# A first phase in fixed order on three engines, and a denser schedule of the late modulation chunks

## The chip, the cores and the metric

The kernel runs on one core of one Trainium2 chip. The metric is the device time of the whole program in microseconds: each run gives one time, and the median over the runs is quoted. Profiled executions give, beside their time, a trace of all engines.

The engines are TensorE (PE in the profile, with its weight loads as PEld), VectorE (DVE), ScalarE (ACT), GpSimd (POOL) and SyncE (SP), which only issues DMAs here.

## The reference

One layer of a diffusion backbone, on 256 latent tokens `x` and 256 context tokens `ctx`, model width 2048, float32 throughout. Cut to what matters:

```python
mod = (silu(c) @ w_mod + b_mod)                    # 6 x 2048: sa, ca, ga, sm, cm, gm
mod_c = (silu(c_ctx) @ w_mod + b_mod)              # only sa_c, ca_c are used
h_c = rmsnorm(ctx, norm_attn_w) * (1 + ca_c) + sa_c
h   = rmsnorm(x,   norm_attn_w) * (1 + ca)   + sa
k_c, v_c = h_c @ w_in[K, V]                        # keys normalized per head
q, k, v, pool_in, gates = h @ w_in                 # q, k normalized, then axial rope
a = softmax(q k^T / 8)[even] - lam * softmax(...)[odd]     # 8 heads, keys of latent and context
y_a = rmsnorm(a @ v) * (1 - lam_init) @ w_a_up
y_b = multiscale_pool(pool_in) @ w_b_up
x = x + ga * ((sigmoid(g_a) * y_a + sigmoid(g_b) * y_b) @ w_o)
x = x + gm * (relu((rmsnorm(x) * (1 + cm) + sm) @ w_ff1) ** 2 @ w_ff2)
```

## The kernel before, in words

**Precision.** Every float32 product with a large weight is made of three matmuls in a reduced format: weight and activation are each split into a high part (a cast on ScalarE) and a low part (a subtraction on VectorE), and high x high, high x low and low x high are summed. A 512 KB weight chunk therefore costs one cast and one subtraction of 128 x 1024 before TensorE uses it.

**Loading.** `stream` is the list of all weight chunks in the order of use, filled by `plan` at the head of the program. `wchunk` gives out the next chunk, and first issues loads on SP's queue until a few chunks lie ahead (`AHEAD` 2, in the first phase `FIRST_AHEAD` 6). Raw chunks go to a few rotating buffers, so SP's queue stops where a buffer is still in use.

**Order.** The program is written as one stream of operations; a planner with its own cost model and priorities puts them into an order for each engine. Operations that go through `pin` keep their written order among themselves. The wrappers `act` and `vec` pin everything while `ordered[0]` is true, and `pe` while `ordered_pe[0]` is true. In the first phase only `ordered_pe` is set before the change.

**First phase.** It computes sa and ca for latent and context, the modulated activations of both, and for the first four heads the keys of latent (`kx`) and context (`kc`) and the queries of latent (`q`), for one 128-row feature tile f of 16 after the other. For each f: `mod_tile(f)` multiplies four raw chunks of w_mod by the two conditioning vectors (32 matmuls) and transposes the result in blocks on VectorE (`blocks`); `features(f)` turns it upright on TensorE (`modT`, L67) through `mod_columns`, scales the activations on VectorE (`hw`), adds the shift on ScalarE for the high part (`hL`, `hC`) and on VectorE for the low part (`hidden`); `product(n, f)` is six matmuls for each of kx, kc, q. `keep` splits a chunk of w_k and w_q at every even f. The norm of the latent tokens is taken at the start; that of the context (`context_squares`, `context_norm`, with one matmul into `ssq`) behind `mod_tile(2)`. Features lag one tile behind mod tiles, context products two. `tables()` makes the rope tables and lambda, behind f = 10. Six PSUM banks accumulate through all of the phase.

**Later phases.** Behind it come values (`v_group(0)`), the other half of queries, keys and values, pooling, and then `gates()`, beside attention as a side generator; then w_o in four column groups of eight chunks; then the MLP. On the way from w_o to the MLP stands a chain: `projected` (xtmp, x, x1sq), `norm2`, `shifted`, transposes `hidden2` (h2T), and the first products in `ff1_first`, written for the first half of the tokens ahead of the second.

**Late modulation.** ga, cm, sm and gm (latent only) are computed on VectorE in the shadow of the later phases: `late_gen` is a generator that at each call loads one 512 KB chunk and orders a multiply-add into `macc` (L624); behind the 16 chunks of each of eight halves comes a sum over partitions on TensorE (`late`, L643). Calls are handed out by credit: each weight chunk in `stream` carries a `rate`, `load_next` adds it to `credit`, and each whole credit is one call. Behind w_o, `while "gm" not in mods: next(late[0])` makes all calls that are still missing for ga, cm and sm.

Of the kernel before, what the change touches and what calls it, by code (L numbers as in the profile page):

```python
# [14 lines left out]
ALU = mybir.AluOpType  # L15
AX = mybir.AxisListType

P = 128
D = 2048
KT = D // P  # L20
T = 256
# [27 lines left out]
def layer(ctx: ExitStack, tc, a, out):  # L49
# [5 lines left out]
    ordered = [False]  # L55
    ordered_pe = [False]
# [12 lines left out]
    act, vec, pe, sp = Engine(nc.scalar, ordered), Engine(nc.vector, ordered), Engine(nc.tensor, ordered_pe), nc.sync  # L69
# [4 lines left out]
    def work(name, shape=None, dt=F32):  # L74
        return pool.tile(shape or [P, 512], dt, tag="w2", name=name, bufs=9)
# [13 lines left out]
    late = [None]  # L89
    credit = [0.0]  # L90
# [33 lines left out]
    stream = []  # L124

    def plan(name, *idx, rate=0.0):
        stream.append(((name,) + idx, rate))
# [3 lines left out]
    for f in range(KT):  # L131
        for i in range(4):
            plan("w_m", f, i)
            if (f, i) == (9, 0):
                plan("prq")
        if f == 1:
            for i in range(4):
                plan("cT", i)
        if f % 2 == 0:
            plan("w_k", 0, f // 2)  # L140
            plan("w_q", 0, f // 2)
    for n, g, rate in (("w_v", 0, 1.5), ("w_q", 1, 1.0), ("w_k", 1, 1.5), ("w_v", 1, 1.5)):
        for ch in range(8):
            plan(n, g, ch, rate=0.0 if (n, g) == ("w_v", 1) and ch < 3 else rate)
    for g in range(4):
# [4 lines left out]
    for g in range(4):  # L150
        for n, nk in (("w_gb_in", 8), ("w_b", 4), ("w_ga_in", 8), ("w_a", 4)):
            for ch in range(nk):
                plan(n, g, ch, rate=0.55)
                if g == 0 and n == "w_gb_in" and ch in (1, 7):
                    plan("pool_w", 2 if ch == 1 else 3)
    for g in range(4):
        for ch in range(8):
            plan("w_o", g, ch, rate=0.25 if g < 3 else 0.0)
            if g == 0:
                plan("x", ch // 4, ch % 4)  # L160
    for b in range(9):
        if b == 0:
            for k in range(KT):
# [8 lines left out]
    FIRST_AHEAD = 6  # L172
# [9 lines left out]
    done = [0]  # L182
# [12 lines left out]
    def load_next():  # L195
        key, rate = stream[len(loaded)]
        src = a[key[0]]
        for i in key[1:]:
            src = src[i]
        if key[0] == "prq":  # L200
            nc.sync.dma_start(prq, src)
            loaded.append((key, None, None))
            return
        if key[0] in ("cT", "x"):
            dst = cT[:, 4 * key[1]:4 * key[1] + 4, :] if key[0] == "cT" else x1_tile()[:, key[1], key[2] * 512:key[2] * 512 + 512]
            nc.sync.dma_start(dst, src)
            loaded.append((key, None, None))
            return
        n = src.shape[-1]
        if key[0] == "w_m":  # L210
            raw = mod_raw(*key[1:])
            sp.dma_start(raw, src)
            loaded.append((key, raw, raw))
            return
        if key[0] in ("w_k", "w_q") and key[1] == 0:
            raw = pool.tile([P, n], F32, tag="aT", name="raw", bufs=2)
            sp.dma_start(raw, src)
            loaded.append((key, raw, raw))
            return
        raw = raw_chunk(src, n)  # L220
        if key == ("w_ff1a", 0):
            hi, lo = (pool.tile([P, n], F32R, tag="aT", name=nm, bufs=2) for nm in ("hi0", "lo0"))
        elif key == ("w_ff1a", 1):
            halves = [[work(nm, dt=F32R) for nm in ("hi1", "lo1")] for _ in range(2)]
            for h in range(2):
                split(*halves[h], raw[:, h * 512:h * 512 + 512])
            loaded.append((key, *zip(*halves)))
            return
        else:
            hi = pool.tile([P, n], F32R, tag="whi", name="whi", bufs=3)  # L230
            lo = pool.tile([P, n], F32R, tag="wlo", name="wlo", bufs=3)
        act.copy(hi, raw)  # L232
        vec.tensor_sub(lo, raw, hi.bitcast(F32))  # L233
        loaded.append((key, hi, lo))
        credit[0] += rate
        credit_rate[0] = rate
        while credit[0] >= 1.0:
            credit[0] -= 1.0
            if late[0] is not None:
                next(late[0], None)  # L240

    def wchunk(*key, ahead=AHEAD):
        while len(loaded) < min(done[0] + 1 + ahead, len(stream)) or loaded[done[0]][1] is None:
            if loaded and done[0] < len(loaded) and loaded[done[0]][1] is None:
                done[0] += 1
                continue
            load_next()
        got, hi, lo = loaded[done[0]]
        assert got == key, (got, key)
        loaded[done[0]] = None  # L250
        done[0] += 1
        tick()
        return hi, lo

    def split(hi, lo, src):
        act.copy(hi, src)
# [23 lines left out]
    xT = s16("xT", [P, KT, T])  # L280
    cT = s16("cT", [P, KT, T])
# [67 lines left out]
    hL = [pairtile("hL0")]  # L349
    hC = [pairtile("hC0")]  # L350
# [10 lines left out]
    def mod_tile(f, ps):  # L361

        raws = [wchunk("w_m", f, i, ahead=FIRST_AHEAD)[0] for i in range(4)]
        c = (f % 2) * T
        for i in range(4):
            for j in range(4):
                k = 4 * i + j  # L370
                pe.matmul(ps[32 * j:32 * j + 32, c:c + T], cv[:, k, :], raws[i][:, j * T:j * T + T],
                          start=k < 4, stop=k >= 12)
        blocks = work("blocks", [P, T])
        vec.transpose(blocks, ps[:, c:c + T])
        return blocks.rearrange("p (a g r) -> p a g r", a=2, g=4)
# [11 lines left out]
        vec.tensor_scalar(c3[:, 0, :], c3[:, 0, :], pr("nw")[:, f:f + 1], None, ALU.mult)  # L387
        return c3

    def hidden(f, t, c3):  # L390

        src, h = ((xT, hL), (cT, hC))[t]
        u = work("hw", [P, T])
        ht, k8 = h[f // 8], f % 8
        bias = c3[:, 1, t:t + 1]
        vec.scalar_tensor_tensor(u, src[:, f, :], c3[:, 0, t:t + 1], rms[t], ALU.mult, ALU.mult)
        act.activation(ht[:, 0, k8, :], u, AF.Identity, bias=bias)
        vec.scalar_tensor_tensor(ht[:, 1, k8, :], u, bias, ht[:, 0, k8, :].bitcast(F32), ALU.add, ALU.subtract)

# [81 lines left out]
    def product(n, k):  # L481

        w = "w_q" if n == "q" else "w_k"
        if w not in fb:
            fb[w] = [bank(f"{w}_{t}") for t in range(4 if n != "q" else 2)]
        hi, lo = held[w, k // 2]
        kk = k % 2
        for t in range(2):
            t4 = t + (2 if n == "kc" else 0)
            xmm([fb[w][t4]], [tokens(4)[t4]], k, hi, lo, slice(kk * 512, kk * 512 + 512), k == 0, k == KT - 1)  # L490
# [13 lines left out]
            total.append(sq[0])  # L504


    ordered_pe[0] = True
    sb = bank("ssq")
    for i in range(4):
        square_sums(xT, vec, sb, i)()  # L510
# [3 lines left out]
    def features(f):  # L514

        if f == 8:
            hL.append(pairtile("hL1"))
            hC.append(pairtile("hC1"))
        cols[f] = mod_columns(f, blocks[f])
        hidden(f, 0, cols[f])  # L520
        for k in (0, 1, 2) if f == 2 else (f,) if f > 2 else ():
            hidden(k, 1, cols[k])

    def context_norm():

# [6 lines left out]
    def keep(w, j, raw):  # L532

        if w == "w_k":
            if not first:
                first.append(s16("first", [P, 4, 1024], F32R))
            i = 2 * (j % 2)
            held[w, j] = first[0][:, i, :], first[0][:, i + 1, :]
        else:
            held[w, j] = [pool.tile([P, 1024], F32R, tag=tag, name=tag, bufs=3) for tag in ("whi", "wlo")]  # L540
        split(*held[w, j], raw)

    for f in range(KT):
        if f % 2 == 0:
            ps = bank("mod")
        if f > 0:
            features(f - 1)
        blocks[f] = mod_tile(f, ps)
        if f == 2:
            for i in range(4):  # L550
                context_squares(i)
            context_norm()
        if f > 0:
            product("kx", f - 1)
        if f == 4:
            for k in range(2):
                product("kc", k)
        if 3 < f < KT - 1:
            product("kc", f - 2)
        if 0 < f < KT - 1:  # L560
            product("q", f - 1)
        if f % 2 == 0:
            for w in ("w_k", "w_q"):
                keep(w, f // 2, wchunk(w, 0, f // 2, ahead=FIRST_AHEAD if f < 14 else 1)[0])
        if f == 10:
            tables()
    features(KT - 1)
    product("kc", KT - 3)
    product("q", KT - 2)
    product("kc", KT - 2)  # L570
    for n in ("kx", "q", "kc"):
        product(n, KT - 1)
    ordered_pe[0] = False
    kb, qb = fb["w_k"], fb["w_q"]
    qT = s8("qT", [P, NH, T])
    kT = s16("kT", [P, NH, 2 * T])
# [591 lines left out]
```

## Time and profile before

| | |
|---|---|
| runs | 1484.52, 1485.43, 1487.09 us, median 1485.43 |
| profiled execution | 1486.54 us, its span 1484.7 us |
| busy in the span | PE 1444.8, PEld 1186.5, DVE 998.6, ACT 686.1, POOL 120.3 us |
| loaded from HBM | 344.45 MB |
| mean granted TensorE clock | 0.989 |

The span runs from the first to the last instruction of the trace; the execution's own time lies 1.8 us above it. Busy times of different engines overlap. In the lines below, a row of waits reads "engine line waited for: us in total, times, longest us"; a row of the chain "start, us, what"; a row of the timeline "start, us, engine line op out<-in xcount [idle before <-what ended it]". All are microseconds from the start of the span. A helper's line (L67, L256, L257) stands for many callers, so tiles are named as well.

### The profile page before, as it was taken

The numbers are of one execution on the slowest core, as the hardware profiler recorded it, in microseconds if no ns is written. First come the engines' busy times: TensorE is split into PE (matmuls) and PEld (weight loads), VectorE is DVE, ScalarE is ACT, GpSimd is POOL, SyncE is SP. The second block draws the span as 40 slices with busy tenths as digits, with TensorE's granted clock in tenths as the row PEclk, the third lists the DMA queues.
The fourth block names the chain that finished last, engine by engine and source line by source line (L and its number), as shares of the span: only waits on it lengthen the run. The fifth ranks groups of instructions, "written<-read, shape, count | busy, mean of one in ns | idle before, by whom it ended". The sixth has DMA issues, their size and how long they took to land.

```text
span 1484.7 us, 19763 instructions
## 1 busy us (share of the span) xinstructions
PE 1444.8 (97%) x7466; PEld 1186.5 (80%) x7466; DVE 998.6 (67%) x1243; ACT 686.1 (46%) x929; POOL 120.3 (8%) x120
## 2 busy tenths in 40 slices
PE   5899999999999999999989999999999999999998
PEld 2567887778888888888858888888888888888887
DVE  3557686858888677777786765666666555555675
ACT  4224345456654444444434545535445453544432
POOL 0000101002400000000000100100000000000260
PEclk8899999999999999999999999999999999999999
DMA  9896494334688888897756677767777565565564
GB/s 378 349 390 257 148 321 156 128 118 159 198 305 300 301 285 286 294 322 249 236 194 215 227 238 239 236 221 236 243 233 247 188 187 196 185 196 188 186 198 141
DMA packets 97439, 347.85 MB, mean 234 GB/s; under 512 B 11072, under 2 KB 11712, under 8 KB 97344
## 3 DMA queue, kind: packets, MB, share of 16 engines
q1 hardware_dynamic: 96768, 345.51, 68.7%
q8 instruction: 58, 0.95, 0.3%
q0 software_dynamic: 576, 1.08, 0.2%
q14 instruction: 37, 0.30, 0.1%
HBM read 344.45 MB, written 2.10 MB: 233 GB/s over the span
## 4 chain that ended last, share of the span: by engine, by line
PE 91%; DVE 4%; DMA 3%; ACT 1%; issue 1%; POOL 0%; SPq 0%; DVEq 0%; ACTq 0%; POOLq 0%
PE f L1017 14%; PE f L427 8%; PE f L426 8%; PE f L429 8%; PE f L1020 7%; PE pg L426 4%; PE pg L427 4%; PE pg L429 4%; PE w_k L67 3%; DMA raw<-in_w_m_dram 2%; PE pyy L426 2%; PE pyy L427 2%; PE pyy L429 2%; PE wo L426 2%; PE wo L427 2%; PE wo L429 2%
## 5 line engine op out<-in xcount | busy, mean ns | idle before, releaser
L233 DVE TENSOR_TENSOR wlo<-raw,whi 128x1024 fp32r<-128x1024 f32 (+1 forms) x433 | 540.0, 1248 | 355.7 <-ACT whi L232 330.7
L232 ACT CAST whi<-raw 128x1024 fp32r<-128x1024 f32 (+1 forms) x433 | 453.3, 1047 | 558.8 <-PE f L427 178.5
L1017 PE MATMUL f<-h,whi 128*128 128x512 f32 x896 | 224.3, 392 | 0.0
L427 PE MATMUL f<-whi,act 128*128 128x512 f32 x512 | 199.3, 389 | 0.0
L426 PE MATMUL f<-whi,act 128*128 128x512 f32 x512 | 199.3, 389 | 0.0
L1017 PEld LDWEIGHTS f<-h,whi 128*128 128x128 f32 x896 | 161.6, 189 | 29.2
L624 DVE SCALAR_TENSOR_TENSOR macc<-raw,sil,macc 128x1024 f32<-128x1024 f32 x128 | 163.9, 1280 | 1.1 <-DMA raw<-in_w_sm_dram 0.7
L429 PE MATMUL f<-wlo,act 128*128 128x512 f32 x512 | 136.8, 389 | 0.0
L1020 PEld LDWEIGHTS f<-h,wlo 128*128 128x128 f32 x896 | 122.2, 190 | 8.7
L1020 PE MATMUL f<-h,wlo 128*128 128x256 f32 x896 | 124.9, 282 | 0.0
L429 PEld LDWEIGHTS f<-wlo,act 128*128 128x128 f32 x512 | 96.1, 188 | 19.9
L427 PEld LDWEIGHTS f<-whi,act 128*128 128x128 f32 x512 | 96.1, 188 | 19.9
L426 PEld LDWEIGHTS f<-whi,act 128*128 128x128 f32 x512 | 96.1, 188 | 19.8
L426 PE MATMUL pg<-whi,hL 128*128 128x512 f32 x256 | 100.7, 393 | 0.0
L427 PE MATMUL pg<-whi,hL 128*128 128x512 f32 x256 | 99.7, 389 | 0.0
L1028 POOL TENSOR_TENSOR rsq<-relu 128x512 f32<-128x512 f32 x28 | 29.1, 1040 | 538.7 <-ACT relu L1027 518.4
L429 PE MATMUL pg<-wlo,hL 128*128 128x512 f32 x256 | 68.4, 389 | 0.0
L427 PEld LDWEIGHTS pg<-whi,hL 128*128 128x128 f32 x256 | 48.1, 188 | 10.2 <-issue 0.2
L426 PEld LDWEIGHTS pg<-whi,hL 128*128 128x128 f32 x256 | 48.1, 188 | 10.2 <-ACT whi L232 0.2
L429 PEld LDWEIGHTS pg<-wlo,hL 128*128 128x128 f32 x256 | 48.0, 188 | 10.0
L426 PE MATMUL wo<-whi,mix 128*128 128x512 f32 x116 | 45.2, 390 | 0.0
L427 PE MATMUL wo<-whi,mix 128*128 128x512 f32 x116 | 45.1, 389 | 0.0
(269 smaller groups left out, 2050.2 us busy)
## 6 DMA issues: line engine op xcount, KB each, us to landing
raw<-in_w_ff_dram SPq DMA_DIRECT2D x240, 512.0 KB, 4.2
raw<-in_w_m_dram SPq DMA_DIRECT2D x64, 512.0 KB, 8.9
raw<-in_w_ga_dram SPq DMA_DIRECT2D x32, 512.0 KB, 4.5
raw<-in_w_cm_dram SPq DMA_DIRECT2D x32, 512.0 KB, 4.7
raw<-in_w_gb_in_dram SPq DMA_DIRECT2D x32, 512.0 KB, 4.7
raw<-in_w_ga_in_dram SPq DMA_DIRECT2D x32, 512.0 KB, 4.8
raw<-in_w_sm_dram SPq DMA_DIRECT2D x32, 512.0 KB, 4.6
raw<-in_w_o_dram SPq DMA_DIRECT2D x32, 512.0 KB, 4.5
```

The source lines that it names most:

```text
L67: return (lambda *a, **k: pin(emit(*a, **k))) if self.flag[0] else emit
L232: act.copy(hi, raw)
L233: vec.tensor_sub(lo, raw, hi.bitcast(F32))
L426: pe.matmul(banks[t], tok(h, k, 0, tt), wt, start=k == 0, stop=False)
L427: pe.matmul(banks[t], tok(h, k, 1, tt), wt, start=False, stop=False)
L429: pe.matmul(banks[t], tok(h, k, 0, tt), wt, start=False, stop=k == 2 * nk - 1)
L624: pin(vec.scalar_tensor_tensor(acc, raw, sil[:, 0, k:k + 1], acc, ALU.mult, ALU.add))
L1017: pe.matmul(ps, hi[:, kk * P:kk * P + P], both(h2, k), start=k == 0, stop=False)
L1020: pe.matmul(ps[:, T:2 * T], lo[:, kk * P:kk * P + P], act_slice(h2, k, 0), start=False, stop=k == KT - 1)
L1028: gp.tensor_mul(sq, r, r)
```

## The change

It touches the first phase and the rates.

- In the first phase ScalarE and VectorE keep the written order too, not TensorE alone.
- The context tokens cT are loaded behind the first modulation tile instead of the second, and their squares and norm stand behind `mod_tile(0)` instead of `mod_tile(2)`.
- Features of tile f stand behind the products of tile f - 1 at the end of a step, for latent and context together; the context product lags one tile, as the others do. Tile 0 has its latent features first and its context features (`hidden_context`) behind the split of the first w_k and w_q chunks; kx and q of tile 0 stand in step 0, kc of tile 0 in step 1.
- `tables()` stands behind f = 11 instead of 10.
- `first_chunk` loads no chunk of the next phase ahead.
- Credit is collected only once the generator exists. The rate of the first w_v group is 0.75 instead of 1.5, that of gates 0.6 instead of 0.55, that of w_o 0.5 in two column groups instead of 0.25 in three. x is loaded two pieces per column group of w_o instead of all eight in the first.

```diff
-        if f == 1:
+        if f == 0:
             for i in range(4):
                 plan("cT", i)
...
-    for n, g, rate in (("w_v", 0, 1.5), ("w_q", 1, 1.0), ("w_k", 1, 1.5), ("w_v", 1, 1.5)):
+    FIRST_LOADS = len(stream)
+    for n, g, rate in (("w_v", 0, 0.75), ("w_q", 1, 1.0), ("w_k", 1, 1.5), ("w_v", 1, 1.5)):
...
-                plan(n, g, ch, rate=0.55)
+                plan(n, g, ch, rate=0.6)
...
-            plan("w_o", g, ch, rate=0.25 if g < 3 else 0.0)
-            if g == 0:
-                plan("x", ch // 4, ch % 4)
+            plan("w_o", g, ch, rate=0.5 if g < 2 else 0.0)
+            if ch % 4 == 0:
+                plan("x", ch // 4, g)
...
-        credit[0] += rate
+        credit[0] += rate if late[0] is not None else 0.0
...
+    def first_chunk(*key):
+        return wchunk(*key, ahead=min(FIRST_AHEAD, FIRST_LOADS - done[0] - 1))[0]
...
-    def hidden(f, t, c3):
-
-        src, h = ((xT, hL), (cT, hC))[t]
+    def hidden(f, c3):
+
+        us = []
+        for t, src in enumerate((xT, cT)[:len(rms)]):
+            u = work("hw", [P, T])
+            vec.scalar_tensor_tensor(u, src[:, f, :], c3[:, 0, t:t + 1], rms[t], ALU.mult, ALU.mult)
+            us.append(u)
+        for t, u in enumerate(us):
+            add_shift(f, t, u, c3)
+
+    def hidden_context(f, c3):
+
         u = work("hw", [P, T])
-        ht, k8 = h[f // 8], f % 8
+        vec.scalar_tensor_tensor(u, cT[:, f, :], c3[:, 0, 1:2], rms[1], ALU.mult, ALU.mult)
+        add_shift(f, 1, u, c3)
+
+    def add_shift(f, t, u, c3):
+
+        ht, k8 = (hL, hC)[t][f // 8], f % 8
         bias = c3[:, 1, t:t + 1]
-        vec.scalar_tensor_tensor(u, src[:, f, :], c3[:, 0, t:t + 1], rms[t], ALU.mult, ALU.mult)
         act.activation(ht[:, 0, k8, :], u, AF.Identity, bias=bias)
         vec.scalar_tensor_tensor(ht[:, 1, k8, :], u, bias, ht[:, 0, k8, :].bitcast(F32), ALU.add, ALU.subtract)
...
-    ordered_pe[0] = True
+    ordered_pe[0] = ordered[0] = True
...
-        hidden(f, 0, cols[f])
-        for k in (0, 1, 2) if f == 2 else (f,) if f > 2 else ():
-            hidden(k, 1, cols[k])
+        hidden(f, cols[f])
...
-        if f > 0:
-            features(f - 1)
         blocks[f] = mod_tile(f, ps)
-        if f == 2:
+        if f == 0:
+            features(0)
             for i in range(4):
                 context_squares(i)
             context_norm()
-        if f > 0:
-            product("kx", f - 1)
-        if f == 4:
-            for k in range(2):
-                product("kc", k)
-        if 3 < f < KT - 1:
-            product("kc", f - 2)
-        if 0 < f < KT - 1:
-            product("q", f - 1)
+        elif f == 1:
+            product("kc", 0)
+            features(1)
+        else:
+            for n in ("kx", "q", "kc") if f < KT - 1 else ("kx", "q"):
+                product(n, f - 1)
         if f % 2 == 0:
             for w in ("w_k", "w_q"):
-                keep(w, f // 2, wchunk(w, 0, f // 2, ahead=FIRST_AHEAD if f < 14 else 1)[0])
-        if f == 10:
+                keep(w, f // 2, first_chunk(w, 0, f // 2))
+        if f == 0:
+            hidden_context(0, cols[0])
+            product("kx", 0)
+            product("q", 0)
+        if f > 1:
+            features(f)
+        if f == 11:
             tables()
-    features(KT - 1)
-    product("kc", KT - 3)
-    product("q", KT - 2)
-    product("kc", KT - 2)
-    for n in ("kx", "q", "kc"):
-        product(n, KT - 1)
-    ordered_pe[0] = False
+    for n, k in (("kc", KT - 2), ("kx", KT - 1), ("q", KT - 1), ("kc", KT - 1)):
+        product(n, k)
+    ordered_pe[0] = ordered[0] = False
```

More of the change, by code (lines that the diff above doesn't have):

```diff
@@ L238, in load_next @@
             credit[0] -= 1.0
-            if late[0] is not None:
-                next(late[0], None)
+            next(late[0], None)
     def wchunk(*key, ahead=AHEAD):
@@ L361, in mod_tile @@
     def mod_tile(f, ps):
-        raws = [wchunk("w_m", f, i, ahead=FIRST_AHEAD)[0] for i in range(4)]
+        raws = [first_chunk("w_m", f, i) for i in range(4)]
         c = (f % 2) * T
```

## The prediction

> **What bounds the kernel now.** I read the busy line of the page first, then TensorE's waits over the whole span, then busy time by stretches around those waits, then the chain of work and the timeline there.
>
> ```profile
> PE 1444.8 (97%) x7466; PEld 1186.5 (80%) x7466; DVE 998.6 (67%) x1243; ACT 686.1 (46%) x929; POOL 120.3 (8%) x120
> ...
> PE ssq L67 <- DVE sq L527: 7.7, 1, 7.7
> PE ssq L67 <- DVE sq L474: 6.9, 1, 6.9
> PE mod L67 <- DMA raw<-in_w_m_dram: 6.3, 8, 2.2
> PE h2T L932 <- DVE yt L67: 4.3, 2, 3.6
> PE qkT L461 <- ACT e L697: 2.5, 1, 2.5
> ```
>
> TensorE bounds the kernel: 1444.8 of 1484.7 us, so all idle time is 39.9 us. An edit that removes no matmul can win only that, and the time matmuls run at half clock behind an idle stretch. Two places hold most of it: the first phase (the ssq and mod waits) and the passage from w_o to the MLP (h2T). The qkT wait lies in attention, which the change leaves alone.
>
> ```profile
> 34.00:42.00 8.00, 0.32 (x5) 0.16 (x1) 7.42 (x11) 3.11 (x4) 0.00 (x0) 0.50 1.03 410
> 42.00:47.00 5.00, 5.00 (x12) 3.94 (x13) 1.27 (x3) 0.98 (x2) 0.00 (x0) 0.51 1.03 409
> ...
> 750.00:760.00 10.00, 6.87 (x28) 4.69 (x26) 7.89 (x10) 3.38 (x8) 1.44 (x2) 1.00 0.91 344
> 760.00:770.00 10.00, 6.93 (x19) 4.56 (x20) 7.73 (x19) 4.12 (x8) 0.00 (x0) 0.66 0.00 1
> ...
> GB/s 150 344 415 418 412 407 411 403 411 411 410 407 407 412 405 241 28 368 403 417 412 404 393 389 316 395 401 375 398 414 404 407 412 411 346 57 224 68 90 98
> ...
> 33.14 1.05 PE L67 MATMUL mod<-raw,cv 128*32 128x256 f32 x8 [0.64 <-DMA raw<-in_w_m_dram]
> ```
>
> Columns of the windows: length, busy time of PE, PEld, DVE, ACT, POOL, granted clock, DMA share, GB/s. From 34 to 42 us TensorE stands still while VectorE squares the context (sq L527 ends the wait), and the five us behind it run 12 matmuls at clock 0.51, 0.42 us each. The GB/s row covers 0 to 150 us in 40 slices of 3.75 us: about 410 GB/s, with one hole near 60 us (28), where buffers still held by late products blocked the loads. At 410 GB/s a 512 KB chunk takes 1.28 us. The mod row says that chunk 22.3 in queue order (prm counted 0.3) has landed by 33.1 us: the stream starts at about 4.6.
>
> ```profile
> 108.75 0.18 PE modT L67 x8
> ...
> 119.90 1.36 PE w_q L67 x6
> 121.26 0.17 PE modT L67 x8
> ...
> 127.65 1.75 PE mod L67 x32
> ...
> 138.19 1.36 PE w_k L67 x6
> 139.55 0.23 PE v L426
> ```
>
> These are pieces of the chain. Two steps of f take 121.26 - 108.75 = 12.51 us: 6.255 each, all TensorE's (a mod tile 1.75, three products of 1.36, modT 0.18, remainder between them). The last mod tile starts at 127.65 and the value projection at 139.55: I measure the first phase by that start.
>
> **The change, first phase.** cT's four chunks move on SP's queue ahead of w_k, w_q and the second modulation tile, which land 4 x 1.28 = 5.1 us later. The whole phase loads 88.9 chunks: 4.6 + 88.9 x 1.28 = 118.4 us for the last one if the queue never stalls, against a mod tile that now starts at 127.65. So loads leave room, and the question is when TensorE gets into its 6.255 us steps.
>
> ```profile
> 17.25 0.48 DVE L396 SCALAR_TENSOR_TENSOR hw<-xT,col,rms 128x256 f32<-128x256 f32 x1
> 17.57 1.04 ACT L256 CAST whi<-raw 128x1024 fp32r<-128x1024 f32 x1 [2.89 <-DMA raw<-in_w_q_dram]
> 18.65 1.22 DVE L257 TENSOR_TENSOR wlo<-raw,whi 128x1024 fp32r<-128x1024 f32 x1 [0.92 <-ACT whi L256]
> 29.63 3.21 ACT L499 ACTIVATE sq<-cT 128x512 f32<-128x512 f32 x6
> 39.57 0.68 DVE L502 TENSOR_TENSOR sq<-sq 128x512 f32<-128x512 f32 x1
> 41.87 1.19 PE L67 MATMUL ssq<-sq,mean 128*128 128x256 f32 x2 [7.68 <-DVE sq L527]
> 45.07 0.42 DVE L273 SCALAR_TENSOR_TENSOR rms<-rq_t,rms 128x256 f32<-128x256 f32 x1
> 121.50 0.16 DVE L386 TENSOR_TENSOR col<-modT,prm 128x4 f32<-128x4 f32 x1 [3.48 <-PE modT L67]
> 123.42 0.48 DVE L398 SCALAR_TENSOR_TENSOR hC<-hw,col,hC 128x256 fp32r<-128x256 f32 x1
> ```
>
> *Start.* Latent features of tile 0 stay where they are: hw at 17.25, hL on ScalarE until 18.3. In fixed order the eight squares of cT follow: 8 x 0.535 (3.21 / 6) ends at 22.6, behind the last cT chunk (4.6 + 12.3 x 1.28 = 20.3). The last adds take about 2.2 behind it: 24.8. From ssq's start to rms ready the rows give 45.49 - 41.87 = 3.6: 28.5. The two casts of w_k and w_q queue behind that on ScalarE, the two subtractions on VectorE end at 28.5 + 2 x 1.22 = 30.9, and hC of tile 0 at 32.4. TensorE, idle until w_k's split, takes kx and q of tile 0 at half clock: five matmuls of 0.42 from 29.7 (31.8), six more, 34.3. Then mod(1). The row of 42 to 47 shows about 5 us of half clock behind an idle stretch; here, with waits in the window, I take it to last until 38: mod(1) at 2 x 1.75 = 3.5 ends at 37.8. At full clock follow kc(0) 1.36, modT 0.18, mod(2) 1.75, three products 4.08, modT 0.18: mod(3) starts at 45.4. It has landed by 4.6 + 28.3 x 1.28 = 40.8.
>
> *The clock.* The Trainium skill, page "TensorE: Matmul & The Clock Gate", section "What's actually happening", gives full speed after one busy window of about 3.4 us. The 42 to 47 row disagrees with it by some 1.6 us; by the rule full clock would come at 29.7 + 3.4 = 33.1, mod(1) would end at 35.5, and the total be some 2.3 us lower than my sum.
>
> *Steps.* mod(15) would start at 45.4 + 12 x 6.255 = 120.5. In a step VectorE's features last from 121.50 to 123.90, 2.4 us, then come the transpose (0.44), and in even steps two subtractions (2.44): all within 6.255, so fixed order costs nothing there; if w_q came over about 1 us late behind its modulation tile, the features behind it would be late by the rest. One step does not fit:
>
> ```profile
> 87.81 0.18 DVE L328 COPY wkt<-prq 128x64 f32<-128x64 f32 x1
> ...
> 89.17 0.28 DVE L339 TENSOR_TENSOR tabs<-prq 128x32 f32<-128x32 f32 x2
> ...
> 99.18 0.32 DVE L343 TENSOR_TENSOR lm<-prq 128x64 f32<-128x64 f32 x2
> ...
> 101.05 0.15 DVE L347 TENSOR_SCALAR nlam<-nlam 128x1 f32<-128x1 f32 x1
> ```
>
> tables() is 1.64 us (87.81 to 89.45), plus 0.65 for lm and its sum, 0.35 for nlam and a round trip to ScalarE's Exp, say 0.7: 3.3. Now it was put into gaps in two places; in fixed order it stands behind features(11), with transpose(12), two subtractions and features(12) queued behind it. Features 2.7 after modT, tables 6.0, transpose 6.4, casts (behind Exp on ScalarE) and subtractions 9.0, hL(12) 10.3, where kx(12) is due at 6.255 + 1.9 = 8.2: TensorE waits 2.1. Bounds: 0 if that tile has slack, 3.3 if all of it shows. So mod(15) starts at 122.6.
>
> *Tail.* Behind mod(15): 1.75, kx and q of 14 (2.72), modT 0.18, kc(14) in the shadow of the features (1.9), three last products 4.08: 10.6 us, value projection at 133.2. Gain 139.55 - 133.2 = 6.3; bounds 0, if the steps lose it, and 11.3, if clock and tables cost nothing (rivals). The w_v loads, no longer issued from within the phase, stand behind the last w_m and land from 118.4 on, 15 us before use; their casts queue behind hC(15) on ScalarE, with 4 us in hand. I take 0, at most 1 of loss.
>
> **The change, late modulation.** Counting credit: before, six w_v chunks are loaded while there is no generator, so calls by the end of w_o are 3 + 8 + 12 + 7.5 + 8 + 96 x 0.55 + 24 x 0.25 = 97.3. gm exists at call 103, so six are forced behind w_o, five of them with a load and a multiply-add. After: 6 + 8 + 12 + 7.5 + 8 + 96 x 0.6 + 8 x 0.5 = 103.1 by the first quarter of w_o, and 107.1 by its half; then rate 0. Nothing is forced.
>
> ```profile
> 400.00:500.00 100.00, 100.00 (x456) 83.01 (x455) 81.01 (x85) 50.64 (x61) 7.39 (x9) 1.00 0.85 293
> ...
> 749.66 1.52 PE L67 MATMUL wo<-wlo,mix 128*128 128x512 f32 x6
> 753.74 1.52 PE L67 MATMUL wo<-wlo,mix 128*128 128x512 f32 x6
> ...
> 751.34 3.93 DVE L624 SCALAR_TENSOR_TENSOR macc<-raw,sil,macc 128x1024 f32<-128x1024 f32 x3 [0.75 <-DMA raw<-in_w_sm_dram]
> ...
> 757.17 0.68 DVE L67 TENSOR_TENSOR xtmp<-wo,ga_bc 128x512 f32<-128x512 f32 x1
> ...
> 761.39 0.69 PE L932 MATMUL h2T<-prm,yt 128*128 128x128 f32 x2 [3.59 <-DVE yt L67]
> ...
> 773.15 0.44 PE L932 MATMUL h2T<-prm,yt 128*128 128x128 f32 x2 [0.75 <-DVE yt L67]
> ```
>
> w_o's first token half ends at 751.18 (749.66 + 1.52), but xtmp, which needs only that, starts at 757.17, behind three forced multiply-adds and their sums. The chain from xtmp to h2T is 4.22. With nothing forced xtmp starts at about 751.8 and h2T at 756.0, against 761.39: 5.4 earlier, 0.7 behind w_o's end (755.26). That wait is too short to halve the clock (0.66 in the row of 760 to 770), which gives up to 1.9 more before the second token half's h2T at 773.15; part is eaten by the next waits there, on casts and norm2: 0.6. Gain 6.0, between 4.5 (those waits grow) and 7.3.
>
> The price of the earlier chunks: five more multiply-adds of 1.3 us in 290 us of gates raise VectorE from 81 to 83%, and loads likewise; the cover is TensorE's full 100 of 100 us, and slack stays. In w_o's first half one late chunk more per four weight chunks is balanced by x's loads, now two a quarter. POOL gets one memset and one small bias load earlier, with nothing waiting. 0, bounds 0 and 1. In attention late chunks move by three calls, which may lift or deepen the 2.5 us qkT wait: plus or minus 2.5.
>
> **Sum.** 6.3 + 6.0 = 12.3 off the profiled execution's 1486.54 (span 1484.7 and 1.8 around it): 1474.2. The median shown, 1485.43, is 1.1 lower than that execution, so against it, and predicted, 1473.1.
>
> **Rivals.**
> (a) A faster first phase: full clock comes as soon as kx of tile 0 is through (q 1.2 and mod(1) 1.75 shorter, 2.9) and tables cost nothing (2.1): 1468.1. For it: the clock's windows run freely. Against: the ssq wait still leaves a gap before 28.
> (b) The first phase gains nothing: fixed order takes from each step what lag and tail give, 0.5 us in each of twelve steps: 1479.4. For it: VectorE's idle before casts in the old trace came from such waits. Against: 2.4 + 0.44 + 2.44 is under 6.255.
> (c) The passage behind w_o keeps its wait, because norm2 and shifted alone are the chain and casts for ff1a stand in VectorE's queue ahead of xtmp: 1479.1. Against: the chain's 4.22 has 4.1 of products beside it.
> (d) Slower: in even steps w_q lands late, its subtraction blocks features on VectorE, and the late subtraction holds the w_k and w_q buffers, so that SP's queue stops behind them. It decides from 12.3 / 8 = 1.5 us in each of eight even steps; at 2 us: 1489.1. For it: one such hole of 5 us stands in the GB/s row. Against: one tile of lag frees those buffers earlier.
>
> **How the numbers follow.** Forecast 0.60, (a) 0.13, (b) 0.11, (c) 0.08, (d) 0.08. The forecast's own range is 1469.5 to 1477.5. To hold 8 in 10 I reach from near (a), 1467.5, to beyond (b) and (c), 1481. A measurement tells about 0.2%, 3 us: faster 0.89, same 0.04, slower 0.07; part of (d) stays within 0.2%.
>
> **What the new profile would show.** Value projection starting at 130 to 136 us; no ssq wait on sq L527 over 4 us but a wait on the splits near 29; no hole in GB/s near 60; a wait of about 2 us on hL or blocks in the step behind tables; steps of 6.26 elsewhere. Behind w_o: no late matmuls, first h2T under 1.5 us behind the last wo, clock near 1.00. The prediction is wrong if even steps last over 7 us, or if the h2T wait stays above 3.

## The result, and the profile after

The changed kernel takes 1474.11 us, the median of four runs (1472.52 to 1475.86), against 1486.11 (four runs, 1484.52 to 1487.09) for the kernel before: a ratio of 0.9921, 95% interval 0.9903 to 0.9938, or 12.0 us less. The prediction was 1473.1, range 1467.5 to 1481. The profiled executions differ by 10.7 us (1486.54 and 1475.86; the second is the slowest of its four), and the stages below add up to that.

First the line of busy time, from the page of the changed kernel:

```profile
span 1474.0 us, 19772 instructions
PE 1440.5 (98%) x7466; PEld 1186.7 (81%) x7466; DVE 1000.8 (68%) x1243; ACT 684.3 (46%) x929; POOL 121.3 (8%) x120
```

The instruction counts are those of before. TensorE's idle time is now 1474.0 - 1440.5 = 33.5 us instead of 39.9; the other 4.3 us of the difference are busy time, which half clock and the modelled ends of matmuls both change, so I go by markers below. Next TensorE's waits in the changed kernel (us in total, times, longest):

```profile
PE ssq L67 <- DVE sq L67: 15.6, 2, 8.3
PE qkT L477 <- ACT e L709: 2.5, 1, 2.5
PE w_k L67 <- ACT first L67: 2.0, 1, 2.0
PE w_k L67 <- ACT hL L67: 1.8, 1, 1.8
PE f L263 <- ACT whi L67: 1.4, 1, 1.4
PE late L655 <- ACT ah L259: 1.1, 1, 1.1
...
PE late L656 <- DVE al L260: 0.8, 1, 0.8
PE w_k L67 <- DVE first L67: 0.8, 1, 0.8
```

Two rows of before are gone, mod on its loads (6.3) and h2T on yt (4.3). The two ssq waits are about as long as they were (15.6 against 14.6). New are the splits (`first`, 2.0 and 0.8), hL behind `tables()` (1.8) and, not foreseen at all, two waits of the late sum (`late`, 1.1 and 0.8), which lie in the gates. Busy time by stretches of the changed kernel (length, busy PE, PEld, DVE, ACT, POOL, granted clock, DMA share, GB/s):

```profile
34.00:42.00 8.00, 8.00 (x88) 4.79 (x88) 3.90 (x9) 2.80 (x4) 0.00 (x0) 0.94 1.02 408
42.00:47.00 5.00, 5.00 (x54) 3.25 (x53) 3.72 (x9) 0.91 (x2) 0.00 (x0) 1.00 1.00 370
400.00:500.00 100.00, 98.09 (x432) 80.37 (x431) 80.52 (x82) 46.14 (x53) 2.55 (x4) 0.98 0.88 294
750.00:760.00 10.00, 7.47 (x29) 5.09 (x28) 9.05 (x20) 5.28 (x11) 0.00 (x0) 0.93 0.05 10
760.00:770.00 10.00, 9.54 (x45) 7.57 (x43) 6.42 (x16) 2.56 (x5) 0.00 (x0) 0.90 0.44 150
```

The stretch of 34 to 42, in which TensorE stood still before, now runs 88 matmuls; 760 to 770 has 9.54 us of work instead of 6.93 and a clock of 0.90 instead of 0.66. The stretch of 400 to 500 was full before and now lacks 1.9 us, at clock 0.98.

The same markers in both traces, in the order of the program, tell where the time went:

| marker on TensorE | before | after | earlier by | stage |
|---|---|---|---|---|
| first low-part matmul of the value projection | 143.18 | 135.22 | 8.0 | first phase: 8.0 won |
| first matmul of the gates (pg) | 394.72 | 385.98 | 8.7 | attention and pooling: 0.8 won |
| last pyy, end of the gates | 667.32 | 662.65 | 4.7 | gates: 4.1 lost |
| last wo | 755.26 | 751.54 | 3.7 | w_o: 0.9 lost |
| last h2T | 804.62 | 793.9 | 10.7 | passage to the MLP: 7.0 won |
| last f | 1480.16 | 1469.46 | 10.7 | MLP: nothing |

These are single executions, and a stage of one can differ from the next by 1 to 2 us without any edit. The first modulation tile already started 0.8 earlier here (12.80 against 13.56), while the same first phase started it at 12.54 and 15.30 in two other executions (after_again and gates_055 below), by when the first loads landed.

**First phase.** The chain of work of the changed kernel, from the context's norm on:

```profile
24.21 1.23 PE ssq L67 x2
...
27.78 1.23 DVE first L67
29.05 2.50 PE w_k L67 x5
31.55 2.56 PE w_q L67 x6
34.11 2.26 PE mod L67 x32
...
44.38 1.75 PE mod L67 x32
...
103.15 1.45 DVE tabs L67 x12
...
110.22 1.71 PE w_k L67 x6
...
121.07 1.75 PE mod L67 x32
...
133.18 0.23 PE v L442
```

These are the prediction's steps: ssq at 24.2 (24.8 foreseen), the splits, products of tile 0 at half clock, mod(1), mod(3) at 44.4 (45.4), steps of 6.22 us, `tables()` with the wait before 110.22, mod(15) at 121.1 (122.6), the uninterrupted value projection at 133.18 (133.2). From 44.38 to 121.07 the chain is TensorE's but for the step behind `tables()`. The GB/s row of the changed kernel over 0 to 150 us, 40 slices:

```profile
GB/s 143 370 413 415 413 409 407 412 406 413 404 402 352 399 418 404 409 410 409 407 409 405 412 406 409 409 411 406 411 375 398 416 395 194 175 9 144 140 138 13
```

The hole near 60 us (241, 28) is gone; behind the first slice the lowest of the stream is 352, and the stream ends near 123 us.

**Behind w_o.** TensorE's timeline there:

```profile
750.02 1.52 PE L67 MATMUL wo<-wlo,mix 128*128 128x512 f32 x6
751.68 0.44 PE L944 MATMUL h2T<-prm,yt 128*128 128x128 f32 x2
...
757.25 0.73 PE L263 MATMUL f<-whi,h 128*128 128x512 f32 x2 [1.41 <-ACT whi L67]
```

The first transpose follows 0.1 us behind the last product of w_o, where it came 6.1 behind. What is late next is a cast for ff1 (1.4).

**Gates.** The chain of work in the stretch where the late sum waits:

```profile
427.80 1.28 DVE macc L636
...
430.81 1.23 DVE wlo L234
432.07 5.42 DMA raw<-in_w_ga_in_dram
...
437.58 1.06 ACT whi L233
438.67 1.10 DVE wlo L234
...
439.81 0.69 DVE al L260
...
440.55 0.50 PE late L656
...
441.34 0.43 PE pg L443
```

A weight chunk of the gates lands late (5.42 us of DMA in the chain). Its load starts as the subtraction of an earlier chunk ends (430.81 + 1.23 = 432.04), and that subtraction came behind a late multiply-add (macc). Its own cast and subtraction stand on ScalarE and VectorE ahead of the casts that the late sum needs; TensorE waits for that sum, and behind it pg runs at 0.43 us a matmul instead of 0.23, at half clock. Nearly all of the gates' loss lies in this place: from 420 to 450 us TensorE works 28.09 of 30 us at a mean clock of 0.94, and in the rest of the gates it is never idle.

### The profile page after: what moved, and what is told of

The parts are those of the page before. It is cut to its first block, busy times and chain, and to the rows that moved or that the text cites. A ratio compares the mean times of both kernels' runs of the same rounds, so it can differ in the third digit from the quotient of the medians.

```text
span 1474.0 us, 19772 instructions
## 1 busy us (share of the span) xinstructions
PE 1440.5 (98%) x7466; PEld 1186.7 (81%) x7466; DVE 1000.8 (68%) x1243; ACT 684.3 (46%) x929; POOL 121.3 (8%) x120
## 4 chain that ended last, share of the span: by engine, by line
PE 88%; DVE 6%; ACT 2%; DMA 2%; issue 1%; POOL 0%; DVEq 0%; SPq 0%; ACTq 0%; POOLq 0%
PE f L1029 14%; PE f L443 8%; PE f L442 8%; PE f L445 8%; PE f L1032 7%; PE pg L443 3%; PE pg L442 3%; PE pg L445 3%; PE w_k L67 3%; PE wo L442 2%; PE wo L445 2%; PE wo L443 2%; PE pyy L445 2%; PE pyy L442 2%; PE pyy L443 2%; DVE wlo L234 2%
## 5 line engine op out<-in xcount | busy, mean ns | idle before, releaser
L1029 PEld LDWEIGHTS f<-h,whi 128*128 128x128 f32 x896 | 161.8, 189 | 29.6
L617 POOL MEMSET macc<- 128x1024 f32 x8 | 7.6, 955 | 461.6 <-DVE al L260 357.1
L442 PE MATMUL wo<-whi,mix 128*128 128x512 f32 x116 | 45.2, 390 | 0.0
```

Of the source, the lines that this page charges most:

```text
L442: pe.matmul(banks[t], tok(h, k, 0, tt), wt, start=k == 0, stop=False)
L617: gp.memset(acc, 0.0)
L1029: pe.matmul(ps, hi[:, kk * P:kk * P + P], both(h2, k), start=k == 0, stop=False)
```

## The experiments

The kernels of each study ran beside the kernel before on the same chip; its median was 1486.77 us for the first four below, 1486.28 for the next four, 1486.44 for the last three.

**The two parts, each alone.** late_only is the old kernel with nothing but the new rates and x's spread loads:

```diff
-                plan(n, g, ch, rate=0.55)
+                plan(n, g, ch, rate=0.6)
...
-            plan("w_o", g, ch, rate=0.25 if g < 3 else 0.0)
-            if g == 0:
-                plan("x", ch // 4, ch % 4)
+            plan("w_o", g, ch, rate=0.5 if g < 2 else 0.0)
+            if ch % 4 == 0:
+                plan("x", ch // 4, g)
```

> The kernel before, with nothing of the change but the rates (gates 0.6, w_o 0.5 in two column groups) and x's loads spread. Theory 1 (the parts add up; late chunks forced behind w_o cost the passage 6 to 7 us, the denser rate in gates costs some 4 us of waits there): first h2T 0.2 to 1 us behind the last wo matmul, a wait of 1 to 2 us on a late sum or on a weight load in gates, time 2 to 4 us under before. Theory 2 (the passage got shorter because the phase before it ran earlier, or the wait in gates is chance): no gain behind w_o, time within 1.5 us of before; or no wait in gates and 6 to 7 us under before.

Measured: 1482.99 us, ratio 0.9975 (0.9966 to 0.9985), 3.8 us less. Its waits of TensorE:

```profile
PE pg L426 <- ACT whi L232: 1.0, 1, 1.0
...
PE h2T L932 <- DVE yt L67: 0.8, 1, 0.8
...
PE late L644 <- DVE al L257: 0.6, 1, 0.6
```

By the markers of its profiled execution (1484.44 us) the passage wins 7.7 us, and the gates and w_o lose 2.9 and 0.9. The first phase, which the edit leaves alone, ended 1.7 later than in the kernel before, which I put down to the spread of single executions.

first_only is the changed kernel with the old rates and x's loads as before (0.375 for w_v, as credit there now counts from another point):

```diff
-    for n, g, rate in (("w_v", 0, 0.75), ("w_q", 1, 1.0), ("w_k", 1, 1.5), ("w_v", 1, 1.5)):
+    for n, g, rate in (("w_v", 0, 0.375), ("w_q", 1, 1.0), ("w_k", 1, 1.5), ("w_v", 1, 1.5)):
...
-                plan(n, g, ch, rate=0.6)
+                plan(n, g, ch, rate=0.55)
...
-            plan("w_o", g, ch, rate=0.5 if g < 2 else 0.0)
-            if ch % 4 == 0:
-                plan("x", ch // 4, g)
+            plan("w_o", g, ch, rate=0.25 if g < 3 else 0.0)
+            if g == 0:
+                plan("x", ch // 4, ch % 4)
```

> The changed kernel, with the rates of before for gates, w_o and x's loads, and a rate of 0.375 in the first w_v group, so that as many late calls are made by each phase as before (97.3 by the end of w_o, six forced). Theory 1: the first phase keeps its 8 us, the passage behind w_o its 3 to 4 us wait on h2T, no wait on late sums in gates: time 7 to 9 us under before, first phase as in the changed kernel. Theory 2 (the passage is shorter whatever the rates): time 12 to 15 us under before.

Measured: 1478.11 us, 0.9938 (0.9925 to 0.995), 8.7 us less. Its waits:

```profile
PE ssq L67 <- DVE sq L67: 15.9, 3, 8.2
PE h2T L944 <- DVE yt L67: 4.3, 2, 3.6
```

The parts add up: 3.8 + 8.7 = 12.5, against 11.7 and 12.0 for both in two studies. The h2T wait falls from 4.3 to 0.8 with the rates alone, and the first h2T follows 0.1 us behind w_o. And the rates bring their own cost, with the old first phase as with the new: late_only has a new wait in the gates (1.0) and one of the late sum (0.6), first_only has none in the gates (its late sum waits 1.2 behind w_o, where the forced calls are).

**The gates' rate.** The changed kernel with the old rate in the gates, and the calls that are then missing made in one more quarter of w_o:

```diff
-                plan(n, g, ch, rate=0.6)
+                plan(n, g, ch, rate=0.55)
...
-            plan("w_o", g, ch, rate=0.5 if g < 2 else 0.0)
+            plan("w_o", g, ch, rate=0.5 if g < 3 else 0.0)
```

> The changed kernel with the old rate of 0.55 in gates and 0.5 in three column groups of w_o, so that gm still exists before w_o ends (102 calls by chunk 16 of w_o). Theory 1 (the 1.9 us of waits at the late sum in gates, and the half clock behind it, come from the denser rate): these waits go, time 3 to 4 us under the changed kernel. Theory 2 (the wait comes from where the sum falls, not from the rate): a wait of 1 to 2 us remains on some late sum, time within 1 us of the changed kernel.

Measured: 1472.03 us, 0.9898 (0.9883 to 0.9913): 14.7 us under the kernel before, where the changed kernel lies 12.0 under it. Its busy time in the stretch in which the changed kernel lost 1.9 us:

```profile
400.00:500.00 100.00, 100.00 (x450) 82.67 (x450) 79.87 (x82) 47.07 (x54) 2.56 (x4) 1.00 0.87 299
```

TensorE is full again. How long the gates last is read from the view of one tile, pg: duration of one in ns (least, median, most), then first and last start. Before, changed, and with the old rate:

```profile
L426 PE MATMUL pg<-whi,hL x256: 387/389/791, 394.7 to 654.9; 128*128 128x512 f32 x128
```

```profile
L442 PE MATMUL pg<-whi,hL x256: 387/389/791, 386.0 to 650.2; 128*128 128x512 f32 x128
```

```profile
L442 PE MATMUL pg<-whi,hL x256: 387/389/791, 386.2 to 646.4; 128*128 128x512 f32 x128
```

That is 260.2, 264.2 and 260.2 us. From the start of the first to the end of the last pg, all five kernels with 0.55 (before, first_only, this one, best and best_attn below) take 261.7 us, and all eight with 0.6 take 263.2 to 266.4, late_only 264.55 among them. So it is the edit of the rate that costs 1.5 to 4.7 us, whatever the first phase does.

By which way it costs is less clear. In the seven kernels with 0.6 and the new first phase, TensorE's waits in the gates lie at one late sum, between 437 and 442 us, but for one of 0.5 (after_again). The rate also moves that sum: here its matmuls come at 443.8 and 447.0, and wait for nothing. Whether the denser loads cost by themselves, or only because a sum now meets a late chunk, was not separated.

**Fixed order itself.** ScalarE and VectorE left to the planner, the rest of the change kept:

```diff
-    ordered_pe[0] = ordered[0] = True
+    ordered_pe[0] = True
```

> The changed kernel, but ScalarE and VectorE keep no written order in the first phase (TensorE does); all else of the change stays. Theory 1 (the gain of the first phase is from earlier context work and one tile of lag, fixed order itself costs 1.8 us at tables): time of the changed kernel minus 0 to 2 us, no 1.8 us wait in the step behind tables. Theory 2 (fixed order is what wins: without it the planner puts splits and squares in wrong places): waits of 1 to 5 us back on ACT hL or on the context squares, time 3 to 8 us over the changed kernel.

Measured: 1474.92 us, 0.9916 (0.9903 to 0.9929), the same as the changed kernel. The wait behind `tables()` is gone, and in its place stand 0.6 on the low part of hL and 1.3 instead of 0.8 on the first split. Fixed order on the two engines wins nothing that can be measured here; the new written order wins without it.

**The changed kernel once more**, as the base of the next three.

> The changed kernel once more, beside the three that follow, so that they are compared on one chip. Expected as measured, 1473 to 1475.5 us; in the profile the waits of 1.1 and 0.8 us at the late sum in gates, 1.8 us behind tables.

Measured: 1474.59 us, 0.992 (0.9906 to 0.9933). The waits are those of the first profile within 0.4 us: 0.7 and 0.9 at the late sum, 1.8 behind `tables()`.

**The wait behind tables().** Only the tables are left to the planner:

```diff
         if f == 11:
+            ordered[0] = False
             tables()
+            ordered[0] = True
```

> The changed kernel, with only the operations of tables() freed from the written order of ScalarE and VectorE. Theory 1 (in fixed order tables stands ahead of transpose, splits and features of tile 12 and shows as a wait of 1.8 us before kx of tile 12): this wait goes, time 1.5 to 2 us under the changed kernel. Theory 2 (the first phase is held by the loads there, so TensorE would wait for the next modulation tile instead): wait on hL gone, but waits on w_m of the same sum, time within 0.5 us.

Measured: 1472.6 us, 0.9911 (0.9898 to 0.9925), 2.0 us under the changed kernel of the same study, though the intervals overlap. In the trace the wait (1.8) is gone, and the step with the tables lasts 6.25 us from one modulation tile to the next (107.39 to 113.64), where the repeated kernel takes 8.20 (106.43 to 114.63): 1.95 saved. The value projection's first matmul comes only 0.8 earlier (126.57 instead of 127.37), since this execution's first modulation tile already started 1.0 later (13.55 against 12.54). The two profiled executions differ by 2.0 as well, but partly by luck: behind the first phase, attention took 1.7 more and the gates 2.5 less in this execution (pg 263.96 against 266.4), which the edit does not touch.

**The start: products or modulation tile first.** kx and q of tile 0 move behind mod(1):

```diff
         elif f == 1:
-            product("kc", 0)
+            for n in ("kx", "q", "kc"):
+                product(n, 0)
...
-            product("kx", 0)
-            product("q", 0)
```

> The changed kernel, but kx and q of tile 0 stand behind the second modulation tile instead of ahead of it. Theory 1 (TensorE waits 2.8 us for the split of the first w_k while the second modulation tile lands at about 27.5 us): these 2.0 and 0.8 us waits are filled in part, mod(2) starts 1 to 2.5 us earlier, time 1 to 2.5 us under. Theory 2 (the modulation tile lands so late that the order makes no difference): waits on w_m of the same sum, time within 0.5 us.

Measured: 1474.03 us, 0.9922 (0.9908 to 0.9936): no change. mod(3) starts 3.6 us earlier (40.48 against 44.10), but the value projection only 0.9 earlier. The summary line of its chain of work from 30 to 125 us:

```profile
by line: DMA raw<-in_w_m_dram 54.5%; PE w_k L67 17.4%; PE w_q L67 8.7%; PE mod L67 8.1%; issue 1.7%; DVE tabs L67 1.5%; DVE wlo L67 1.3%; PE modT L67 1.1%; ACT first L67 1.1%; ACT hL L67 1.1%; DVE hw L67 1.0%; DVE col L67 0.8%; DVE hL L67 0
```

Loads now make up 54.5% of the chain: at some 410 GB/s the phase can't run much faster, so a saving at its start beyond the change's is mostly given back before the end, as theory 2 has it.

**The clock.** 48 matmuls without use keep TensorE at work while the context's squares are made:

```diff
             features(0)
+            wb = bank("warm")
+            for i in range(48):
+                pe.matmul(wb[:, 0:T], ones, hL[0][:, 0, 0, :], start=True, stop=True)
```

> The changed kernel with 48 more matmuls (ones by the high part of tile 0, 256 columns, into a bank that nobody reads) behind the latent features of tile 0, where TensorE waits 8.3 us for the context norm. Theory 1 (the prediction's clock term: the wait halves the clock for kx, q and mod(1), some 2.5 us lost): granted clock 1.00 from about 28 on, mod(2) 2 to 2.9 us earlier, time 2 to 3 us under the changed kernel. Theory 2 (behind the wait the splits and the second modulation tile set the pace, not the clock): clock 1.00, but waits on wlo or w_m in its place, gain under 1 us.

Measured: 1474.23 us, 0.9918 (0.9904 to 0.9931): no change. Its stretches:

```profile
24.00:26.00 2.00, 2.00 (x18) 1.90 (x16) 0.92 (x2) 0.00 (x0) 0.00 (x0) 1.00 1.02 399
26.00:28.00 2.00, 0.30 (x2) 0.00 (x0) 0.58 (x2) 1.63 (x3) 0.00 (x0) 1.00 1.03 412
28.00:30.00 2.00, 0.58 (x2) 0.27 (x2) 1.97 (x4) 1.24 (x2) 0.00 (x0) 0.90 1.02 408
30.00:32.00 2.00, 2.00 (x5) 1.62 (x6) 1.42 (x3) 0.51 (x1) 0.00 (x0) 0.50 0.98 344
32.00:34.00 2.00, 2.00 (x7) 1.35 (x6) 0.46 (x1) 0.00 (x0) 0.00 (x0) 0.75 0.93 311
```

The clock is full from 24 to 28, and lost again while TensorE waits for the splits (2.0 and 1.1 us, between 26.3 and 29.9): the products of tile 0 run at 0.50 all the same. mod(2) starts 0.25 us earlier (37.59 against 37.84), no more.

**The lag.** The context product two tiles behind, as in the old kernel:

```diff
-            product("kc", 0)
...
-            for n in ("kx", "q", "kc") if f < KT - 1 else ("kx", "q"):
-                product(n, f - 1)
+            for n, k in (("kx", f - 1), ("q", f - 1), ("kc", f - 2)):
+                product(n, k)
```

> The changed kernel, with the context product two tiles behind again (kc of f - 2 in step f), all else as changed: fixed order, early context norm, early cT. Theory 1 (the first phase gains from getting the context norm out of its way; the lag only moves 1.4 us of products from step 1 to the tail and holds w_k's buffers a step longer): a hole in the loads or waits on the split of w_k of 0.5 to 1.5 us, time 0 to 2 us over the changed kernel. Theory 2 (the lag is what pays, since its buffers blocked SP's queue near 60 us before): the hole of some 5 us is back, time 4 to 6 us over the changed kernel.

Measured: 1474.5 us, 0.9923 (0.9911 to 0.9935), the same. Its GB/s row, 0 to 150 us:

```profile
GB/s 139 403 417 415 409 411 409 410 400 411 407 407 410 406 409 411 404 410 412 404 408 407 410 406 411 406 411 407 406 412 406 411 351 260 38 69 75 140 140 103
```

No hole near 60 us, with the longer lag too, so the lag did not close it. Without fixed order a shallow dip is left (306 and 342 GB/s in no_fixed_order, against 241 and 28 before). What made the hole is in the trace of the kernel before, ScalarE's timeline:

```profile
59.80 1.05 ACT L256 CAST first<-raw 128x1024 fp32r<-128x1024 f32 x1 [5.04 <-PE w_k L67]
```

The cast of the third w_k chunk waits 5.0 us for TensorE's products with w_k, and SP's queue waits 6.3 us for the subtraction behind that cast. The splits of w_k have two places (`first`), and the first one was still in use: with the context norm behind `mod_tile(2)`, kc of tiles 0 and 1 stood in step 4, together with that of tile 2. The early context norm brings these products into earlier steps, with either lag.

**What the runs point to.** best joins gates_055, tables_free and mod1_first:

> The changed kernel with three edits together: gates at 0.55 and w_o at 0.5 in three column groups, tables() freed from the fixed order, kx and q of tile 0 behind the second modulation tile. Theory 1 (the edits save different waits: 4 us in gates, 1.8 us at tables, 1 us at the start): 1467 to 1470 us, with waits on w_m of 1 to 4 us in the first phase, whose loads then set the pace. Theory 2 (what the first phase saves is taken back by loads altogether): 1470.5 to 1472 us.

Measured: 1467.44 us, 0.9877 (0.9863 to 0.989): 19.0 us under the kernel before and 7 under the changed one. Its waits of TensorE:

```profile
PE ssq L67 <- DVE sq L67: 15.9, 2, 8.3
...
PE mod L67 <- DMA raw<-in_w_m_dram: 1.8, 4, 0.6
```

No late sum, no tables, hardly a split (0.2). With mod(1) run at half clock in front of them, the splits are ready when TensorE wants them; the loads set the pace instead.

best_attn hands some of the late chunks of attention to pooling, against the qkT wait:

```diff
-    for n, g, rate in (..., ("w_v", 1, 1.5)):
+    for n, g, rate in (..., ("w_v", 1, 0.75)):
...
-            plan("w_p", 2 * g + i // 2, i % 2, rate=0.5)
+            plan("w_p", 2 * g + i // 2, i % 2, rate=0.75)
```

> The kernel of best, with fewer late chunks beside the second value group (0.75 instead of 1.5) and more beside pooling (0.75 instead of 0.5). Theory 1 (the 2.5 us wait of qkT on the softmax comes from late multiply-adds that wait for their loads in VectorE's queue ahead of the row maxima): this wait and the half clock behind it go, 2 to 4 us under best. Theory 2 (VectorE is full there with the heads' own work): wait of 1.5 to 2.5 us remains, time within 1 us of best, or over it by waits in pooling.

Measured: 1470.46 us, 0.9894 (0.9879 to 0.9909), 3.0 us more than best. Its waits:

```profile
PE aTp L724 <- DVE d L819: 3.1, 1, 3.1
...
PE qkT L477 <- ACT e L710: 0.5, 1, 0.5
```

The qkT wait falls from 2.5 to 0.5, so the late multiply-adds beside it were its cause, in the main. But in the chain of work of pooling one of them (1.20 us) now stands two instructions ahead of `d`, and the wait there is longer than the one it replaced.

## Why the prediction was right, and where it was not

The forecast's two mechanisms are what happened, and each is shown alone: first_only wins 8.7 us without the rates, late_only 3.8 without the first phase. The total is within 1.0 us of 1473.1, but partly because errors cancel: by stages, 12.3 was expected as 6.3 + 6.0, and 10.7 came in the profiled execution as 8.0 + 0.8 - 4.1 - 0.9 + 7.0.

- **The step that failed: "0, bounds 0 and 1" for the denser rate in the gates.** It cost 4.1 us in the profiled execution, and 1.5 to 4.7 over the eight kernels with 0.6. The reasoning took TensorE's full 100 of 100 us and VectorE's 81% for slack. Busy share wasn't the limit: VectorE has 80.52 us of work in that stretch, nearly what it had (81.01). The weight chunk came late, and a late load followed by two engines in series, in order, reaches TensorE. Why it came late is shown in part: its load started when a buffer came free, behind a late multiply-add, and in the gates SP's queue stands for the late multiply-adds to free buffers for 55.1 us in the changed kernel, against 43.0 before and 47.7 in gates_055 (for the subtractions of weight chunks, 147 to 160 in each). The stretch moved 294 GB/s where the first phase reaches 410. No run changed the number of buffers. That the edit of the rate is the cause is shown (gates_055, first_only, late_only).
- **First phase, 6.3 expected, 8.0 measured.** The largest mis-sized term is the end of the half clock: taken as 38 us, it was 34.9, so mod(1) took 2.26 instead of 3.5 and mod(3) began 1.0 early. Steps and the wait behind `tables()` gave 0.5 more (1.81 instead of 2.1; steps of 6.22 to 6.25). The tail was right, 10.5 against 10.6: from mod(15) to 133.18 lie 12.1 us, of which 1.6 are seven matmuls of the value projection that the planner put among the last products, and which the marker 139.55 did not have.
- **Passage, 6.0 expected, 7.0 measured, and 0.9 lost ahead of it.** The first h2T came 0.1 behind w_o instead of 0.7, and two stretches of half clock became one (about 760.3 to 767.1 before, 758.5 to 761.9 after), which the 0.6 for the clock undervalued. The late sums' matmuls now stand in w_o: moved, not removed. The step counted the multiply-adds that move and forgot these.
- **What the new profile would show.** Right: value projection between 130 and 136, the wait on the splits near 29 (2.0 until 27.5, 0.8 until 29.05), no hole near 60, about 2 us behind `tables()`, steps near 6.26, h2T under 1.5 us behind w_o. Wrong: "no ssq wait on sq L527 over 4 us". The wait of 8.3 us is still there and only stands from 16 to 24 us, when the stream has delivered few chunks, instead of 34 to 42. By the prediction's own 4.6 + n x 1.28, the four chunks of mod(1) land between 24.2 and 28.0, so TensorE would have had little to do there in any order. Also wrong: a clock near 1.00 behind w_o.
- **The rivals.** (a) had its clock half right and its free tables wrong; tables_free shows what the second part is worth, 1.95 us of its step. (b)'s cause, fixed order taking time from steps, did not occur. (c) is refuted by late_only as well. (d) named a late load that blocks an engine's queue; that is what happened, in the gates and not in the first phase. Its reading of the old hole was right as far as late products go, but not that one tile of lag removes it (lag_two).
- **The rule on the clock.** The prediction set the Trainium skill's page "TensorE: Matmul & The Clock Gate", section "What's actually happening" (full speed after one busy window of some 3.4 us) against the row of 42 to 47 and took the row. Between the 33.1 of the rule and the 38 of the row the clock came at 34.9. The same section says that the window is free-running; with that, rule and rows agree (last section), and the error was to count it from the first matmul.

What stays open: no run moved the context norm alone, so that it closes the hole is read from the trace of before and not tested by itself. The old written order with ScalarE and VectorE fixed wasn't tried.

## What to carry to other kernels

Here a background task shared load buffers and a queue with the main stream, and it cost time while every busy share showed slack: price such a task's rate by the next chunk's landing time, and change the rate alone to see. A single wait that can't be removed costs least where the engine would lack data anyway. And when a change fixes an order and writes a new one, run the new order without the fixing: here the first phase's gain came without it.

## What the runs showed of the hardware

The granted clock halves for whole stretches of about 3.4 us: 441.0 to 444.5 in the changed kernel's gates behind 1.9 us of waits, 758.5 to 761.9 in its passage, 19.4 to 22.8 and 29.6 to 33.0 in warm_48 (the last two worked out from 0.67 in 18 to 22 with 0.62 in 22 to 23, and from 0.90 in 28 to 30 with 0.75 in 32 to 34). Longer ones are near multiples: 17.9 to 34.9 in the changed kernel is five times 3.4, and 33.2 to 46.9 before is four; 760.3 to 767.1 before is two (from 0.57 in 760 to 762 and 0.72 in 766 to 768). So half clock outlasts the idle time by a varying amount: by 3.5 us from the ssq row in best (24.7 to about 28.3), by 5.1 before (41.87 to 46.95), by 5.9 in the changed kernel (29.05 to 34.9), where, as I read it, a wait of 0.8 spoilt one more stretch. This fits the free-running window of 3413 ns that the Trainium skill's page "TensorE: Matmul & The Clock Gate" gives in "What's actually happening". Not expected: waits of 1.9 us together (1.07 and 0.84, at the late sum) were enough to cost such a stretch, 1.7 us on top of the wait. They need not be: in warm_48 the same sum waited 1.53 and 0.84, and the clock stayed at 1.00. Which of the two happens would follow from where the waits lie between the borders of the stretches; no run set that.
